# Norm factors moved from the stored rows to the gathered columns, and the residual made by GpSimd during the first experts

## The chip, the cores and the metric

The kernel runs on one core of one Trainium2 chip. The metric is the device time of one execution in microseconds; the median of several executions is compared. The engines are called PE (TensorE matmul), PEld (its weight load), DVE (VectorE), ACT (ScalarE), POOL (GpSimd) and SP (SyncE, which issues most transfers).

## What is computed

One encoder layer over 512 tokens of width 1024, in fp32: a gated DeltaNet mixer, a layer norm, a mixture of experts, a second layer norm and a gated per-token input. The part that matters here:

```
x  = LN(alpha * x + mixer(x))            # first norm: (t - mean) * rstd * g + b
h  = HierMoE(x)                          # top-1 of 4 groups, top-2 of its 8 experts
x  = LN(alpha * x + h)                   # alpha = 2 ** 0.25
x  = x + sigmoid(x Wg) * (p Wp)
```

Each of the 32 experts is `(silu(x Wgate) * (x Wup)) Wdown` with a hidden width of 256.

## The kernel before

**Up to the first norm.** Tokens lie in 4 chunks of 128 rows; `x1[:, c]` is chunk c (128 x 1024). The mixer's output products (`out_products`, L810) for chunk c are added to `x1[:, c]` by DVE (`stats`, L818), which also makes mean and rstd with a chain of very small instructions. `flip_rows` transposes the raw rows on PE (L835) and ACT copies them out (L837); `logits` (L843 to L846) makes the router's logits from raw rows and corrects them by mean and rstd, so routing does not need the normalised rows. `apply` then normalises the rows in place: chunk 1 on DVE with four two-input instructions (L853, L854), chunks 0, 2 and 3 on ACT (L856) followed by four GpSimd instructions each (L859 multiplies by g, L860 adds b; `lng` holds g and b as four broadcast tiles). `store` writes the rows to a DRAM buffer `x1d` and afterwards multiplies `x1` by alpha on ACT (L865), which makes it the residual that the experts' outputs are added to. In this stage a planner orders the instructions of each engine.

**Routing.** Written order on PE, DVE, ACT and POOL: the one-hots of group and experts (L965 to L999), a prefix count on PE (`prk`, L1004), the sort of tokens into 8 passes of 256 slots, and a table on PE (L1077) whose result `gim` gives the row numbers of the gather. `fetch(0)` (L952) gathers 256 rows of `x1d` by two indirect transfers of the POOL queue. `project_p(c)` (L914 to L918), four matmuls, two ACT copies and two stores for chunk c, is work for the last stage that can be put anywhere; `NPJ` says how many chunks come before `prk`, before the first table and before the rest. Then a second, overflow table follows.

**Experts.** Eight passes q = 0 to 7 in a written order on all engines. A pass has 8 up steps and 4 down steps; each step uses one 1 MB weight tile that holds four experts (`w`). Half of a step's matmuls use `w` itself; the other half need a copy of it in an order that the routing decides: `stage` (L1216, L1218) makes it with three DVE copies and one ACT copy of 128 x 512, into two buffers (`ws`). `flip_x` transposes the gathered rows in four parts (PE L1206) and ACT copies each part to `xgT` (L1207). `add` (L1311, DVE) adds the outputs of pass q to the residual `z` (which is `x1`) during the up steps of pass q + 1. `fetch(q + 2)` is issued after the up steps of pass q. Weight tiles rotate through 16 buffers (`ring`, RA + RB); the transfers wait on SP's queue until a buffer comes free.

Of the kernel before, what the change touches and what calls it, by code (L numbers as in the profile page):

```python
# [7 lines left out]
F32 = mybir.dt.float32  # L8
# [3 lines left out]
AF = mybir.ActivationFunctionType  # L12
OP = mybir.AluOpType
# [3 lines left out]
P = 128  # L17
S = 512
D = 1024
KT = 8  # L20
NC_ = 4
NH = 16
NP = 8
ALPHA = 2.0 ** 0.25
# [10 lines left out]
RA = 9  # L35
RB = 7
# [4 lines left out]
R1 = 14  # L41
R0 = 12
NLB = 3
SPE = 'GGGG'
SO = (1, 2, 0, 3)
TE = 'V'
NPJ = (0, 1, 1)
LNV = (1,)
GE = 'GV'
BKK = 4  # L50
BK = 6
# [14 lines left out]
def program(ctx: ExitStack, tc: tile.TileContext, a: dict, out: bass.AP):  # L66
    nc = tc.nc
    V, A, G, T = nc.vector, nc.scalar, nc.gpsimd, nc.tensor
# [14 lines left out]
    x1 = x1p.tile([P, NC_, D], F32, name="x1")  # L83
    lgp = x1p
# [19 lines left out]
    wk = tr.enter_context(tc.tile_pool(name="wk", bufs=2, side="right"))  # L104
    hd = tr.enter_context(tc.tile_pool(name="hd", bufs=4, side="right"))
# [118 lines left out]
    def after(ins, gate, sync=False):  # L224

        cls = mybir.DependencyClass.Sync if sync else mybir.DependencyClass.NoSync
        tc.add_manual_dep(ins.ins, gate.ins.name, mybir.DependencyInfo(cls, mybir.DependencyReason.DATA),
                          reason="order")
# [35 lines left out]
    kcm, qcm, ktm, nv, kkq = {}, {}, {}, {}, {}  # L264
# [323 lines left out]
    def finish(qt, get):  # L588

        ps = (2 * qt, 2 * qt + 1)  # L590
        ms = wk.tile([P, 2, NC_, 2], F32, name="ms")
        scr = wk.tile([P, P], BF16, name="scr", bufs=1)
        for p in ps:
            for c in range(NC_):
                for e in range(2):
                    A.activation(scr, oacc[p][:, c, e], AF.Square, accum_out=ms[:, p % 2, c, e:e + 1])

        for p in ps:
            V.scalar_tensor_tensor(ms[:, p % 2], ms[:, p % 2], 1.0 / P, nq2[:, :, p:p + 1].to_broadcast([P, NC_, 2]),
                                   op0=OP.mult, op1=OP.add)  # L600
        f = wk.tile([P, 2, NC_, 2], F32, name="ff")
        t = wk.tile([P, 2, NC_, 2], F32, name="rq2")
        rsqrt(f, ms, t)
        for p in ps:
            oa = oacc[p]
            G.tensor_tensor(oa, oa, f[:, p % 2, :, :, None].to_broadcast([P, NC_, 2, P]), op=OP.mult)
        for p in ps:
            oa = oacc[p]
            for e in range(2):
                h = 2 * p + e  # L610
                pt = psum.tile([P, NC_, P], F32, name="pmisc", bufs=1)
                for c in range(NC_):
                    T.transpose(pt[:, c], oa[:, c, e], ident)
                zs = wk.tile([P, S], F32, name="zs")
                nc.sync.dma_start(zs, z_dram[h])
                V.scalar_tensor_tensor(zs, pt.rearrange("p c t -> p (c t)"), nw, zs, op0=OP.mult, op1=OP.mult)
                if p not in get():
                    nc.sync.dma_start(oz_dram[h], zs)
                else:
                    oh, ol = get()[p][e]  # L620
                    A.activation(oh, zs, AF.Copy)
                    V.tensor_tensor(ol, zs, oh.bitcast(F32), op=OP.subtract)
            yield
# [115 lines left out]
    wrg = wk.tile([P, KT, 38], F32, name="dc", bufs=3)  # L739
    nc.sync.dma_start(wrg, a["w_rt"])  # L740
    gwr = [wk.tile([P, KT, 36], F32, name="Q") for _ in range(2)]
    for i in range(2):
        V.tensor_tensor(gwr[i], wrg[:, :, 0:36], wrg[:, :, 36 + i:37 + i].to_broadcast([P, KT, 36]), op=OP.mult)
    psg = psum.tile([P, 2, 36], F32, name="ps3", bufs=1)
    for i in range(2):
        for kt in range(KT):
# [19 lines left out]
    for n in range(4):  # L766
        pt_ = wk.tile([P, 256], F32, name="st", bufs=6)
        nc.sync.dma_start(pt_, a["pe_p"][:, 1, 256 * n:256 * n + 256])
        early_p.append(((lambda w, p: w, 1), 256 * n, 256, pt_))
    lng = [hd.tile([P, S], F32, name="kkq", bufs=BKK) for _ in range(4)]  # L770
    for i in range(4):
        nc.sync.dma_start(lng[i], a["ln"][:, i // 2, 512 * (i % 2):512 * (i % 2) + 512].to_broadcast([P, 512]))

    weave((2, finish(3, lambda: {6: o4[0:2], 7: o4[2:4]}), 0, 0, 0.2), (4, split_w2(), 0, 0, 0.5),
          (8 - F7, fl, 0, 0, 1))
# [7 lines left out]
    def ring(shape, dt=F32):  # L783
        nonlocal turn
        turn += 1
        return (ringa if (turn - 1) % (RA + RB) < RA else ringb).tile(shape, dt, name="w")
# [7 lines left out]
    def load():  # L794

        if len(ready) < len(loads):
            ready.append(ring([P, 4, 512]))
            return nc.sync.dma_start(ready[-1], loads[len(ready) - 1])
# [48 lines left out]

    def apply(c, y, nm, ny):

        if c in LNV:  # L850
            for n in range(2):
                ns = slice(512 * n, 512 * n + 512)
                V.scalar_tensor_tensor(x1[:, c, ns], x1[:, c, ns], nm, lng[n], op0=OP.add, op1=OP.mult)  # L853
                V.scalar_tensor_tensor(x1[:, c, ns], x1[:, c, ns], y, lng[2 + n], op0=OP.mult, op1=OP.add)  # L854
        else:
            A.activation(x1[:, c], x1[:, c], AF.Identity, bias=ny, scale=y)  # L856
            for n in range(2):
                ns = slice(512 * n, 512 * n + 512)
                G.tensor_tensor(x1[:, c, ns], x1[:, c, ns], lng[n], op=OP.mult)  # L859
                G.tensor_tensor(x1[:, c, ns], x1[:, c, ns], lng[2 + n], op=OP.add)  # L860

    def store(c):
        stored.append(nc.sync.dma_start(x1d[c * P:(c + 1) * P, :], x1[:, c]))

        A.activation(x1[:, c], x1[:, c], AF.Copy, scale=ALPHA)  # L865

    stored, ps, xT, mo = [], {}, {}, {}
    for i in range(NC_ + 3):
# [15 lines left out]
    tr.close()  # L884
    ringb = rA.enter_context(tc.tile_pool(name="ringb", bufs=RB, side="left", reuse_waits="tile"))
    early = [load() for i in range(RA, R0)]
    for c in SO:
        store(c)
        if R0 > RA:
            after(stored[-1], early[-1])  # L890
    for i in range(max(RA, R0), R1):
        after(load(), stored[-1])
    per = ctx.enter_context(tc.tile_pool(name="per", bufs=1, side="right", reuse_waits="tile"))

    def layernorm(dst, src, gb, pool):
# [52 lines left out]
    def fetch(q):  # L948

        xg = ab_pool.tile([P, 2, D], F32, name="E")  # L950
        for t in range(2):
            i = nc.gpsimd.indirect_dma_start(out=xg[:, t], out_offset=None, in_=x1d[:, :],  # L952
                                         in_offset=bass.IndirectOffsetOnAxis(ap=gim[:, 2 * q + t:2 * q + t + 1], axis=0))
        fetched.append(i)
        return xg
# [139 lines left out]
        project_p(c)  # L1095
    gim, gfm, numbers = table(s128, col, "m", V if TE == "V" else G)
    xg = [fetch(0)]
    for i in range(R1, RA + RB):
        after(load(), fetched[0], True)
    for c in range(NPJ[2], NC_):  # L1100
        project_p(c)
    numbers()


    jf = t32.rearrange("p k c (i e) -> p (k c) i e", i=4)[:, :, :, 0:3]
# [2 lines left out]
                    op=OP.is_ge)  # L1108
# [89 lines left out]
    def flip_x(xg):  # L1198

        xgT = ab_pool.tile([P, KT, 256], F32, name="AT")  # L1200

        def part(k2):
            pt = PT([P, 2, 256], "pmisc" if k2 == 2 else "ps3")
            for i in range(2):
                for t in range(2):
                    T.transpose(pt[:, i, t * P:(t + 1) * P], xg[:, t, (2 * k2 + i) * P:(2 * k2 + i + 1) * P], ident)  # L1206
            A.activation(xgT[:, 2 * k2:2 * k2 + 2], pt, AF.Copy)  # L1207
        return xgT, [lambda k2=k2: part(k2) for k2 in range(4)]

    def stage(w, js):  # L1210

        ws = ek.tile([P, 4, 512], F32, name="ws", bufs=WS)
        for p in range(4):
            src = w[:, bass.ds(js[p], 1)]
            if ROLE[p] == ENG.DVE:
                V.tensor_copy(ws[:, p:p + 1], src)  # L1216
            else:
                A.activation(ws[:, p:p + 1], src, AF.Copy)  # L1218
        return ws

    def quad(ps, l, w, first, last):
        for j in range(4):
# [90 lines left out]
    def overflow(ot):  # L1313
# [3 lines left out]
        with tc.For_i(0, nv_, 1) as i:  # L1317
# [10 lines left out]
            for n in range(2):  # L1328
                pt = PT([P, 4, P], "pmisc")
                for k in range(4):  # L1330
                    T.transpose(pt[:, k], xg[:, (4 * n + k) * P:(4 * n + k + 1) * P], ident)
                A.activation(xt[:, n].rearrange("p (k t) -> p k t", k=4), pt, AF.Copy)
            pg = PT([P, 512], "ps2")
            for k4 in range(2):
                w = (w0, w1)[k4]
# [124 lines left out]
    for q in range(8):  # L1460
        if q == 0:
            man = in_order()
        js = jss[q]
        if q == 0:
            ws = stage(ready[0], js)
        h = up(q, xgT, js, ws, fill)
        parts = []
        if q < 6:
            xg.append(fetch(q + 2))
        if q < 7:  # L1470
            xgT, parts = flip_x(xg.pop(0))
        ws = stage(ready[12 * q + KT], js)
        hT = []
        for x in h:
            hT.append(flip_h(x))
            if parts:
                parts.pop(0)()
        oh = slots(q)
        ys = []
        if q == 7:  # L1480
            parts = [first]
        ws = down(q, hT, js, ws, parts, ys)
        fill = [lambda q=q, c=c, n=n, y=y, oh=oh: add(q, c, n, combine(oh, y, c, "ps1" if q % 2 else "pin"))
                for n, y in enumerate(ys) for c in range(NC_)]
# [104 lines left out]
```

## Time and profile before

| what | value |
|---|---|
| median of 3 runs | 1117.06 us (1114.53 to 1119.78) |
| profiled execution: its own time / its span | 1118.27 us / 1116.5 us |
| PE busy | 1009.3 us, 90% of the span |
| DVE busy | 809.4 us, 72% |
| ACT busy | 548.3 us, 49% |
| POOL busy | 334.3 us, 30% |
| mean granted TensorE clock | 0.942 of full speed |

The profiled execution is 1.2 us above the median. Busy shares are averages over stages with different limits; the stages here are the norm and routing (from about 700 us to 769 us of the span) and the experts (769 us to about 1045 us).

### The profile page before, as it was taken

Reading aid. Unit: us, or ns where it says so; the run is one execution under the profiler, and the core shown is the slowest. Engines: PE = TensorE matmul, PEld = TensorE weight load, DVE = VectorE, ACT = ScalarE, POOL = GpSimd, SP = SyncE. Lnnn points to the kernel's source line nnn. Section 1 sums busy time; section 2 is a strip of 40 time slices with the busy share of each in tenths; the row PEclk is TensorE's granted clock in tenths of the full one; section 3 lists DMA queues with packets and bytes.
Section 4 is the critical chain, followed back from the end, with each engine's and each line's share of the span. In section 5 each row is a group of like instructions: output and inputs, shape, how many; then the busy total and the mean of one; then the engine's idle time right before and its main releaser. Section 6 shows DMA issues by size and latency. Waiting matters only on the chain. (4 is left out here: it accounts for less than half of the span.)

```text
span 1116.5 us, 19701 instructions
## 1 busy us (share of the span) xinstructions
PE 1009.3 (90%) x6954; PEld 703.5 (63%) x6954; DVE 809.4 (72%) x1834; ACT 548.3 (49%) x1406; POOL 334.3 (30%) x273
## 2 busy tenths in 40 slices
PE   9876798977979999989999999958999999999688
PEld 7755677765868887778877888833333333333377
DVE  5889997999894778996556322697666666666784
ACT  3455566655574777556586343224443334432321
POOL 1544534232234344424240274052000000000452
PEclk7988899987999998999999999969999999999789
DMA  4324232121123313223154234878999999970401
GB/s 150 108 66 124 85 98 65 49 57 29 48 90 124 91 58 117 92 77 111 61 161 145 88 123 132 340 274 309 415 420 419 420 406 393 393 319 38 190 28 48
DMA packets 80117, 188.71 MB, mean 169 GB/s; under 512 B 15345, under 2 KB 36849, under 8 KB 67345
## 3 DMA queue, kind: packets, MB, share of 16 engines
q1 hardware_dynamic: 77712, 179.05, 44.1%
q0 software_dynamic: 2304, 8.39, 2.0%
q8 instruction: 55, 0.90, 0.3%
q14 instruction: 46, 0.37, 0.1%
HBM read 174.77 MB, written 12.65 MB: 168 GB/s over the span
## 5 line engine op out<-in xcount | busy, mean ns | idle before, releaser
L240 POOL TENSOR_TENSOR wl<-wr,wh 128x512 fp32r<-128x512 f32 x120 | 160.8, 1343 | 322.8 <-PE pin L243 136.6
L243 PE MATMUL pin<-xh,wh 128*128 128x512 f32 x448 | 137.1, 426 | 36.1 <-DVE cv L257 29.1
L243 PE MATMUL pin<-xl,wh 128*128 128x512 f32 x448 | 135.2, 419 | 0.0
L243 PE MATMUL pin<-xh,wl 128*128 128x512 f32 x448 | 131.2, 412 | 0.3 <-POOL wl L240 0.3
L243 PEld LDWEIGHTS pin<-xh,wh 128*128 128x128 f32 x448 | 86.4, 202 | 57.6 <-DVE cv L257 12.6
L238 ACT ACTIVATE wh<-wr 128x512 fp32r<-128x512 f32 x120 | 75.8, 632 | 92.5 <-PE pin L243 41.2
L1218 ACT ACTIVATE ws<-w 128x512 f32 x96 | 60.5, 630 | 111.8 <-PE ps L1223 57.9
L1216 DVE COPY ws<-w 128x512 f32 x288 | 105.7, 424 | 9.4 <-issue 3.5
L257 DVE SCALAR_TENSOR_TENSOR cv<-pin,cvw,cv 128x510 f32<-128x510 f32 (+1 forms) x128 | 94.4, 741 | 14.8 <-ACT cv L254 14.0
L243 PEld LDWEIGHTS pin<-xl,wh 128*128 128x128 f32 x448 | 89.1, 202 | 19.4 <-DVE xl L642 0.2
L243 PEld LDWEIGHTS pin<-xh,wl 128*128 128x128 f32 x448 | 87.2, 198 | 19.1 <-POOL wl L240 0.7
L952 POOL DMA_INDIRECT E<-x1d,gim x16 | 16.2, 1013 | 170.3 <-PE ps L1206 157.0
L446 POOL TENSOR_TENSOR dc<-dc,negm 128x512 f32<-128x512 f32 x32 | 47.0, 1473 | 44.3 <-DMA dc<-gcd 18.9
L397 DVE TENSOR_TENSOR x<-x,tmp 128x30 f32<-128x30 f32 (+14 forms) x120 | 56.3, 469 | 2.1
L395 DVE TENSOR_TENSOR tmp<-x 128x30 f32<-128x30 f32 (+14 forms) x120 | 53.5, 446 | 2.1
L1311 DVE SCALAR_TENSOR_TENSOR x<-pin,cq,x 128x512 f32<-128x512 f32 x36 | 26.9, 750 | 36.4 <-PE pin L1306 33.0
L448 ACT ACTIVATE dc<-dc,lb 128x128 f32<-128x128 f32 x128 | 41.6, 399 | 15.2 <-POOL dc L446 14.2
L1435 PE MATMUL ps<-w 128*128 128x512 f32 (+1 forms) x192 | 46.4, 405 | 0.0
L542 DVE SCALAR_TENSOR_TENSOR r<-ps,negc,nv 128x128 f32<-128x128 f32 x96 | 29.0, 344 | 23.3 <-PE ps L539 23.1
L1435 PEld LDWEIGHTS ps<-w 128*128 128x128 f32 x192 | 37.5, 206 | 7.6
L1223 PE MATMUL pin<-ws,AT 128*32 128x512 f32 x256 | 39.8, 593 | 0.8 <-DVE ws L1216 0.8
L538 PE MATMUL ps<-st,kcm 128*128 128x256 f32 x96 | 31.7, 413 | 9.6 <-DVE st L570 5.6
(460 smaller groups left out, 2164.7 us busy)
## 6 DMA issues: line engine op xcount, KB each, us to landing
w<-in_w_gu SPq DMA_DIRECT2D x64, 1024.0 KB, 10.0
w<-in_w_dn SPq DMA_DIRECT2D x32, 1024.0 KB, 8.4
wr<-in_w_in SPq DMA_DIRECT2D x96, 256.0 KB, 2.7
dc<-gcd SPq DMA_DIRECT2D x32, 256.0 KB, 3.4
wr<-in_w_out SPq DMA_DIRECT2D x24, 256.0 KB, 3.0
zd<-th SPq DMA_DIRECT2D x16, 256.0 KB, 2.5
zs<-zd SPq DMA_DIRECT2D x16, 256.0 KB, 2.7
w<-in_pe_g SPq DMA_DIRECT2D x6, 512.0 KB, 5.9
```

The costliest lines, as they stand in the source:

```text
L238: A.activation(wh, wr, AF.Copy)
L240: G.tensor_tensor(wl, wr, wh.bitcast(F32), op=OP.subtract)
L243: T.matmul(ps, w[:, k], parts[k0 + k][n], start=(k0 + k + n == 0 and w is wh), stop=(k0 + k == nk_ - 1 and w is wl))
L257: V.scalar_tensor_tensor(y[:, lo:hi], ps[:, lo + j - 2:hi + j - 2], cvw[:, m, j:j + 1], y[:, lo:hi], op0=OP.mult, op1=OP.add)
L395: V.tensor_tensor(t, X[:, m + 1:, m:m + 1].to_broadcast([P, n, m]), X[:, m:m + 1, :m].to_broadcast([P, n, m]), op=OP.mult)
L397: V.tensor_tensor(X[:, m + 1:, :m], X[:, m + 1:, :m], t, op=OP.add)
L446: G.tensor_tensor(dc, dc, negm[:, d:d + 1].to_broadcast([P, 4, P]), op=OP.add)
L448: A.activation(dc[:, u], dc[:, u], AF.Exp, bias=lb[:, c, u0 + u:u0 + u + 1])
L1216: V.tensor_copy(ws[:, p:p + 1], src)
L1218: A.activation(ws[:, p:p + 1], src, AF.Copy)
L1223: T.matmul(ps[32 * j:32 * j + 32], l[:, 32 * j:32 * j + 32], w[:, j], start=first, stop=last, skip_group_check=True)
L1435: T.matmul(pg[n][:, 0:w], x_[:, kt], w_[kt][:, 512 * n + o:512 * n + o + w], start=(kt == 0 and m == 0), stop=(kt == KT - 1 and m == 2))
```

## The change

Rows are normalised by ACT alone, without g and b, for all four chunks, and stored so. The gathered, transposed columns get g and b instead: `gbT` holds them one value per partition, and each part of `flip_x` is copied by two ACT instructions with a scale and a bias in place of one. The g and b rows for the residual are loaded later into one buffer of the weight ring (`lng`), multiplied by alpha by ACT, and GpSimd makes the residual in 16 instructions (`residual`), placed after the up steps and `fetch(2)` in pass 0. `NPJ` goes from (0, 1, 1) to (2, 3, 3).

```diff
-SO = (1, 2, 0, 3)
-NPJ = (0, 1, 1)
-LNV = (1,)
+NPJ = (2, 3, 3)
@@ finish
-        t = wk.tile([P, 2, NC_, 2], F32, name="rq2")
+        t = wk.tile([P, 2, NC_, 2], F32, name="rq2", bufs=1)
@@ before the output products
+    gbT = lgp.tile([P, KT, 2], F32, name="gbT")
+    V.tensor_copy(gbT, wrg[:, :, 36:38])
-    lng = [hd.tile([P, S], F32, name="kkq", bufs=BKK) for _ in range(4)]
-    for i in range(4):
-        nc.sync.dma_start(lng[i], a["ln"][:, i // 2, 512 * (i % 2):512 * (i % 2) + 512].to_broadcast([P, 512]))
@@ apply
-        if c in LNV:
-            for n in range(2):
-                ns = slice(512 * n, 512 * n + 512)
-                V.scalar_tensor_tensor(x1[:, c, ns], x1[:, c, ns], nm, lng[n], op0=OP.add, op1=OP.mult)
-                V.scalar_tensor_tensor(x1[:, c, ns], x1[:, c, ns], y, lng[2 + n], op0=OP.mult, op1=OP.add)
-        else:
-            A.activation(x1[:, c], x1[:, c], AF.Identity, bias=ny, scale=y)
-            for n in range(2):
-                ns = slice(512 * n, 512 * n + 512)
-                G.tensor_tensor(x1[:, c, ns], x1[:, c, ns], lng[n], op=OP.mult)
-                G.tensor_tensor(x1[:, c, ns], x1[:, c, ns], lng[2 + n], op=OP.add)
+        A.activation(x1[:, c], x1[:, c], AF.Identity, bias=ny, scale=y)
@@ store
-        A.activation(x1[:, c], x1[:, c], AF.Copy, scale=ALPHA)
-    for c in SO:
+    for c in range(NC_):
         store(c)
@@ after the stores and two weight loads
+    lng = ring([P, 4, 512])
+    after(nc.sync.dma_start(lng, a["ln"][:, 0:2].rearrange("o k (n w) -> o (k n) w", n=2).to_broadcast([P, 4, 512])),
+          stored[-1])
@@ routing
-    for i in range(R1, RA + RB):
+    for i in range(R1, RA + RB - 1):
         after(load(), fetched[0], True)
     for c in range(NPJ[2], NC_):
         project_p(c)
     numbers()
+    A.activation(lng, lng, AF.Copy, scale=ALPHA)
@@ flip_x
-            A.activation(xgT[:, 2 * k2:2 * k2 + 2], pt, AF.Copy)
+            for i in range(2):
+                kt = 2 * k2 + i
+                A.activation(xgT[:, kt], pt[:, i], AF.Identity, scale=gbT[:, kt, 0:1], bias=gbT[:, kt, 1:2])
+    def residual():
+        for c in range(NC_):
+            for n in range(2):
+                ns = slice(512 * n, 512 * n + 512)
+                G.tensor_tensor(x1[:, c, ns], x1[:, c, ns], lng[:, n], op=OP.mult)
+                G.tensor_tensor(x1[:, c, ns], x1[:, c, ns], lng[:, 2 + n], op=OP.add)
@@ pass loop, after the up steps and the fetch
+        if q == 0:
+            residual()
```

The same scale and bias are applied in the loop for overflowing slots, which has no iterations with these inputs.

## Rows read from the trace of the kernel before

**Rows 1.** Busy time by stretch, in the experts: us, PE, PEld, DVE, ACT, POOL, clock, DMA share, GB/s.

```profile
850.00:900.00 50.00, 49.50 (x360) 18.66 (x363) 33.78 (x78) 20.64 (x39) 2.02 (x2) 1.00 1.01 412
```

**Rows 2.** Busy time by stretch, end of the norm and routing; same columns.

```profile
724.00:728.00 4.00, 4.00 (x36) 3.87 (x35) 4.00 (x6) 3.30 (x6) 3.27 (x3) 1.00 0.21 41
...
744.00:748.00 4.00, 2.35 (x8) 1.32 (x8) 3.65 (x21) 0.00 (x0) 0.00 (x0) 0.50 1.02 373
```

**Rows 3.** Timeline of PE, norm and routing: start, length, engine, line, operation, count.

```profile
729.31 0.63 PE L835 MATMUL ps<-cst,x 128*128 128x128 f32 x4
...
733.56 1.77 PE L843 MATMUL ps<-Q,zs 128*128 128x36 f32 x8
745.65 0.29 PE L1004 MATMUL ps<-ohs,cb 128*128 128x160 bf16 x1 [10.32 <-DVE ohs L999]
...
746.04 6.03 PE L914 MATMUL pin<-E,AT 128*128 128x512 f32 x8
...
753.02 10.55 PE L914 MATMUL pin<-E,AT 128*128 128x512 f32 x24
```

**Rows 4.** Timeline of DVE, last logits to the gather's row numbers.

```profile
736.13 0.26 DVE L846 SCALAR_TENSOR_TENSOR lg<-lg,ly,gs 128x36 f32<-128x36 f32 x1
...
737.42 1.15 DVE L973 TENSOR_TENSOR ohg<-ohg,kmg 128x16 f32<-128x16 f32 x1
738.68 1.25 DVE L978 TENSOR_TENSOR t<-lg,ohg 128x128 f32<-128x128 f32 x1
...
741.12 1.19 DVE L970 TENSOR_TENSOR oh<-oh,ROW 128x32 f32<-128x32 f32 x1
...
744.75 0.19 DVE L973 TENSOR_TENSOR oh<-oh,km 128x32 f32<-128x32 f32 x1
744.98 0.29 DVE L988 TENSOR_TENSOR OH<-ohg,oh 128x128 f32<-128x128 f32 x1
...
753.66 0.17 DVE L1083 CAST gim<-gfm 128x16 int32<-128x16 f32 x1
```

**Rows 5.** Timeline of POOL and of SP's queue, the norm's last instructions and the stores.

```profile
739.73 3.75 POOL L860 TENSOR_TENSOR x<-x,kkq 128x512 f32<-128x512 f32 x3
...
734.69 9.13 SPq L863 DMA_DIRECT2D x1d<-x  x4
```

**Rows 6.** Timeline of DVE and PE, experts, passes 0 and 1.

```profile
781.84 2.10 DVE L1216 COPY ws<-w 128x512 f32 x6 [1.03 <-PE pin L1223]
...
787.49 0.42 DVE L1233 TENSOR_TENSOR h<-h,pin 128x256 f32<-128x256 f32 x1 [1.89 <-ACT h L1232]
...
830.58 1.04 PE L1223 MATMUL ps<-w,hT 128*32 128x512 f32 x8
831.44 1.04 PE L1223 MATMUL ps<-ws,hT 128*32 128x512 f32 x8
```

**Rows 7.** A DVE copy in the mixer: line's shortest, median, longest (ns), and one timeline case.

```profile
L422 DVE COPY x<-x x16: 395/422/1491, 160.5 to 494.8; 32x512 f32<-32x512 f32 x16
...
164.00 1.49 DVE L422 COPY x<-x 32x512 f32<-32x512 f32 x1
...
163.87 1.33 POOL L240 TENSOR_TENSOR wl<-wr,wh 128x512 fp32r<-128x512 f32 x1 [5.10 <-ACT wh L238]
```

**Rows 8.** Timeline of POOL and DVE in the last norm, both back to back.

```profile
1050.08 5.10 POOL L1406 TENSOR_TENSOR w<-w 128x1024 fp32r<-128x1024 f32 x2 [9.86 <-ACT w L1405]
...
1050.13 2.84 DVE L1421 SCALAR_TENSOR_TENSOR x<-x,ly,E 128x512 f32<-128x512 f32 x1
1052.89 2.83 DVE L1420 SCALAR_TENSOR_TENSOR x<-x,mv,E 128x512 f32<-128x512 f32 x1
```

**Rows 9.** ACT copies out of PSUM by shape (busy, mean ns), and a PE wait in flip_x.

```profile
L1207 ACT ACTIVATE AT<-ps 128x512 f32<-128x512 f32 x6 | 3.6, 595 | 1.1 <-PE ps L1206 0.9
...
L1241 ACT ACTIVATE hT<-pmisc 128x256 f32<-128x256 f32 x16 | 6.1, 382 | 2.9 <-PE pmisc L1239 2.8
L304 ACT ACTIVATE kkq<-pmisc,rk 128x128 f32<-128x128 f32 x64 | 18.3, 369 | 5.9 <-PE pmisc L302 5.8
...
858.24 0.66 PE L1206 MATMUL ps<-cst,E 128*128 128x128 f32 x4 [0.21 <-ACT AT L1207]
```

More of the change, by code (lines that the diff above doesn't have):

```diff
@@ L1331, in overflow @@
                     T.transpose(pt[:, k], xg[:, (4 * n + k) * P:(4 * n + k + 1) * P], ident)
-                A.activation(xt[:, n].rearrange("p (k t) -> p k t", k=4), pt, AF.Copy)
+                    kt = 4 * n + k
+                    A.activation(xt[:, n, k * P:(k + 1) * P], pt[:, k], AF.Identity, scale=gbT[:, kt, 0:1],
+                                 bias=gbT[:, kt, 1:2])
             pg = PT([P, 512], "ps2")
```

## Prediction

> **What bounds the kernel now.** I read the busy shares first, then busy time by stretch around the change, then the timelines of all engines from the last output products to the second pass, and last the groups by shape for prices. Two stages matter, and they have different limits.
>
> In the experts PE is the limit: 49.5 of 50 us busy, with the DMA engines full as well and DVE at 33.8 of 50 [rows 1]. What delays PE there delays the end by as much, because no later stage has room to give it back. DVE is the engine closest behind. Each step of an up or down pass takes PE two groups of eight matmuls, 0.86 us apart [rows 6], so 1.72 us, and needs three DVE copies, which run at 2.10 / 6 = 0.35 us each back to back [rows 6]: 1.05 of 1.72 us, with only two `ws` buffers between the engines.
>
> In the norm and routing the limit changes hands. Until 729.9 PE is full (4.00 of 4 us in 724 to 728, [rows 2]; the last transposes of chunk 3 end at 729.31 + 0.63, [rows 3]). From there DVE is the chain: the last logits end at 736.4, the one-hots let PE start `prk` at 745.65 after 10.32 us of idling, and the gather's row numbers are ready at 753.8 [rows 3, 4]. The stores of the rows are not in that chain: the last of the four is issued by 743.8 [rows 5], ten microseconds ahead of the gather. So storing rows earlier is worth nothing by itself; a faster DVE chain is worth its full length, since gather, overflow table and experts follow it in order.
>
> **What the change takes away.** The DVE chain is slowed by GpSimd. While the norm's GpSimd instructions run (3.75 / 3 = 1.25 us each, [rows 5]), DVE instructions with two tensors in SBUF take about the length of one of these more: L973 1.15 us against 0.19 for a larger one undisturbed, L978 1.25 against 0.29 for L988 of its shape, L970 1.19 against about 0.19 [rows 4]. These three alone hold 0.96 + 0.96 + 1.00 = 2.9 us. All twelve GpSimd instructions and the four DVE instructions of chunk 1 go from this place.
>
> Last logits: PE's transposes still end at 729.9. An ACT copy of 0.60 [rows 9], half of the logits' matmuls (1.77 us on a clock that has fallen, [rows 3]; I take 1.2) and two small DVE instructions (0.5) give 732.2, against 736.4. From logits to one-hots it took 745.65 - 736.4 = 9.25 us; less 2.9 that is 6.35, so the one-hots are ready at 738.6.
>
> The new `NPJ` puts eight of the 16 `project_p` matmuls ahead of `prk` on PE. The trace records each twice: 24 records in 10.55 us are three chunks at full clock, 3.5 us each; 8 records in 6.03 us are one chunk at half clock [rows 3], where the granted clock was 0.50, the lower of the two levels (1.2 GHz), after PE had idled [rows 2, 3]. Two chunks from 731.7 on end at 738.8 at full clock and at 743.8 at half. PE comes to them straight from full work, so I take full clock: `prk` at 738.8 instead of 745.65, **6.9 us gained**. The bounds are 1.9 (half clock) and 8.0 (PE done first, one-hots at 737.6). After `prk` nothing on the chain changes; the other chunks fit into waits there. The one ACT instruction on `lng`, the `gbT` copy, the four g and b loads that leave SP's queue and the later load of `lng` stand ahead of nothing that waits: I cost them at nothing. The weight ring loses a buffer for its first turn; a load that was issued 16 steps ahead is issued 15 ahead, some 25 us before it is needed. If transfers were late the cover would be gone, but PE shows no wait on a weight tile.
>
> **What it adds: the column factors.** Each part of `flip_x` is one ACT copy of 0.597 us; it becomes two of 128 x 256. The trace has a plain one at 0.382 and a scaled one of 128 x 128 at 0.369, which at (0.597 - 0.382) / 256 us per element makes 0.476 for 256 [rows 9]. So a part takes 0.76 to 0.95 us, 0.17 to 0.36 more. PE waits for just this copy once in every pass (0.21 us before the second part's transposes, [rows 9]), so the addition lands on PE: eight flips, 1.4 to 2.9 us. I take **2 us lost**.
>
> **What it adds: the residual.** Sixteen GpSimd instructions of 1.25 us, 20.1 us together, start behind `fetch(2)` about halfway through pass 0's up steps. They are off PE's path, but behind the shared access to SBUF stands DVE. A DVE copy like `stage`'s, single input, SBUF to SBUF, takes 0.42 us and was held to 1.49 when a GpSimd instruction ran from 163.87 to 165.20: it ended 0.3 us behind it [rows 7]. Copies, not only two-input instructions, are blocked. Where both engines had work back to back they took turns: two GpSimd instructions of 2.4 us side by side with DVE's L1421 and L1420, each 2.83 instead of 0.75 or so [rows 8]. Behind the blocked copy on DVE stand the other two of its step, and PE waits for them.
>
> If they take turns one for one, the residual needs 16 x (1.25 + 0.42) = 26.7 us, in which DVE makes 16 copies, 5.33 steps, worth 9.2 us of PE: 17.5 us lost. Between up and down DVE has nothing to copy (idle 1.89 us and a product that reads PSUM, [rows 6]); two GpSimd instructions pass free there, 2.5 us. That leaves **15 us lost**. The bounds: 0, if GpSimd only fills DVE's idle time, and 20.1, if nothing overlaps.
>
> Of this the Trainium skill, SBUF — State Buffer, section "Who interferes with whom", says that a DVE instruction in a two-port mode and a GpSimd instruction exclude each other for the whole instruction, and that issue order decides who waits. By that rule the three copies of a step, if they are issued together, could all go ahead of the next GpSimd instruction; the sum would then be that of the third rival below. [Rows 8] speak for one for one, with two-input instructions; no row shows copies back to back against GpSimd back to back.
>
> **The sum.** From the profiled execution: 1118.3 - 6.9 + 2 + 15 = 1128.4. It stands 1.2 above the median, so the median should come to **1127**. Over bounds: losses of 10 to 17.5 and gains of 4 to 8 make 1121 to 1134, the likeliest case's own range.
>
> **Rivals.**
> 1. *The residual costs nothing* (not slower). GpSimd gets its turns in DVE's idle time, 16 of 50 us [rows 1], and the copies keep PE fed. For it: DVE has this idle time. Against it: [rows 7], a GpSimd instruction once started holds a copy up, and GpSimd has nothing that paces it. Time: 1117.1 - 6.9 + 2 = 1112. It decides as soon as the residual costs PE less than 4.9 us.
> 2. *The routing gain fails too.* The clock falls before the projections and they hold `prk` back: gain 1.9. For it: half clock at that very place before [rows 2]. Against it: that came after PE had idled, and now it has work. Time: 1117.1 - 1.9 + 2 + 15 = 1132.
> 3. *Three copies for each GpSimd instruction.* The residual stretches to 16 x (1.25 + 1.05) = 36.8 us, in which DVE makes 48 copies, 16 steps, 27.5 us of PE: 9.3 lost, less 2.5 at the turn: 6.8. Time: 1117.1 - 6.9 + 2 + 6.8 = 1119. The page named above would allow it.
>
> **Chances.** My forecast 0.55, rival 1 0.22, rival 2 0.10, rival 3 0.13. A measurement of this kernel can tell about 0.5%, 5.6 us, from no change: under 1111.5 is faster, over 1122.6 slower. Rival 1 lies at the edge and is split: 0.12 faster, 0.10 same. Rival 3 is the same in 0.11. The forecast's lower end gives 0.04 to the same. A residue of 0.02 goes to faster, for a routing chain that loses more than I count. That makes 0.14 faster, 0.25 same, 0.61 slower. The range of 8 in 10 reaches from 1111, which leaves out the better half of rival 1, to 1135.
>
> **What the profile would show.** Gain: no GpSimd instruction between 724 and 744, no DVE instruction of routing over 0.6 us but the large one-hots, `prk` near 739, `gim` near 747, the first up matmul near 762. Flip: two ACT instructions of 0.4 to 0.5 us per part, PE's wait at the second part 0.4 to 0.6. Residual: sixteen GpSimd instructions in about 27 us, `stage` copies of some 1.6 us among them, steps of about 5 us on PE where they were 1.7, and then the old rhythm. I am wrong if those copies stay near 0.4 us, or if GpSimd's instructions are the ones that stretch, to several microseconds each.

## The result, and the profile after

The changed kernel takes 1127.62 us (median of nine runs, 1119.53 to 1129.81) against 1117.06 us before (nine runs, 1114.53 to 1120.45). The ratio is 1.0081, with a 95% interval of 1.0055 to 1.0106: slower, by about 9 us. Its profiled execution has an own time of 1128.93 us and a span of 1127.1 us.

In both profiled executions the last output product of the mixer starts on PE at nearly the same moment (724.4 before, 724.3 after), so times from there on can be set side by side. The marks, from the timelines of DVE and PE:

| mark | before | after | difference |
|---|---|---|---|
| last logits ready | 736.4 | 735.7 | -0.7 |
| `prk` starts | 745.65 | 740.94 | -4.7 |
| row numbers `gim` | 753.66 | 749.09 | -4.6 |
| first up matmul of pass 0 | 768.96 | 763.82 | -5.1 |
| first matmul that brings pass 0's outputs back (L1306, after L1307) | 800.55 | 807.19 | +6.6 |
| last group of such matmuls, last pass | 1046.56 | 1055.88 | +9.3 |
| end of the span | 1116.5 | 1127.1 | +10.6 |

So routing gained 5.1 us, pass 0 lost 11.8, the other seven passes lost 2.7, and the last stage 1.3. The border between the first two scatters: the first up matmul comes 39.5 us after the last output product here (44.5 before), but 40.9 to 41.0 in a_no_residual, f_half, i_skew and j_same_op, whose routing is the same.

**Routing.** Busy time by stretch of the changed kernel (us, PE, PEld, DVE, ACT, POOL, clock, DMA share, GB/s), to be read beside [rows 1, 2]:

```profile
724.00:728.00 4.00, 4.00 (x31) 3.39 (x30) 3.14 (x14) 4.00 (x7) 0.00 (x0) 1.00 0.00 0
...
740.00:744.00 4.00, 3.06 (x12) 1.63 (x12) 3.69 (x23) 0.72 (x2) 0.00 (x0) 1.00 0.97 321
748.00:752.00 4.00, 3.91 (x13) 1.84 (x14) 2.11 (x14) 0.00 (x0) 1.56 (x2) 0.50 1.01 415
776.00:798.00 22.00, 17.39 (x96) 4.24 (x88) 20.73 (x17) 8.49 (x16) 21.35 (x17) 1.00 0.90 349
850.00:900.00 50.00, 49.17 (x348) 18.66 (x340) 31.84 (x73) 19.05 (x37) 2.02 (x2) 1.00 0.99 401
```

GpSimd is gone from the norm (0.00 us in 724 to 728). In 776 to 798, while GpSimd makes the residual, PE is busy for 17.39 of 22 us only. Timeline of PE in the changed kernel, answering to [rows 3]:

```profile
727.12 3.60 PE L904 MATMUL pin<-E,AT 128*128 128x512 f32 x8
...
735.79 3.70 PE L904 MATMUL pin<-E,AT 128*128 128x512 f32 x8 [0.69 <-ACT ws L907]
740.94 0.23 PE L994 MATMUL ps<-ohs,cb 128*128 128x160 bf16 x1 [1.44 <-DVE ohs L989]
...
763.82 1.94 PE L1224 MATMUL pin<-w,AT 128*32 128x512 f32 x8 [1.20 <-ACT AT L1200]
```

Timeline of DVE from the last logits, answering to [rows 4]:

```profile
735.43 0.26 DVE L844 SCALAR_TENSOR_TENSOR lg<-lg,ly,gs 128x36 f32<-128x36 f32 x1
...
736.72 0.17 DVE L963 TENSOR_TENSOR ohg<-ohg,kmg 128x16 f32<-128x16 f32 x1
737.00 0.38 DVE L968 TENSOR_TENSOR t<-lg,ohg 128x128 f32<-128x128 f32 x1
...
749.09 0.17 DVE L1073 CAST gim<-gfm 128x16 int32<-128x16 f32 x1
```

The same instructions that took 1.15 and 1.25 us in [rows 4] take 0.17 and 0.38. But a `project_p` chunk (727.12, 3.60 us) now stands on PE among the last transposes and logits, so the last logits come hardly earlier than before. From them to `prk` it takes 5.3 us where it took 9.25.

**Pass 0.** Timeline of POOL in the changed kernel (the first three and the last of the sixteen residual instructions):

```profile
776.19 1.29 POOL L1219 TENSOR_TENSOR x<-x,w 128x512 f32<-128x512 f32 x1
777.56 1.34 POOL L1220 TENSOR_TENSOR x<-x,w 128x512 f32<-128x512 f32 x1
778.86 1.44 POOL L1219 TENSOR_TENSOR x<-x,w 128x512 f32<-128x512 f32 x1
...
797.21 1.32 POOL L1220 TENSOR_TENSOR x<-x,w 128x512 f32<-128x512 f32 x1
```

Timelines of DVE (nine copies in one row, then a copy out of that row in a narrower stretch) and of PE in the same time:

```profile
775.80 13.29 DVE L1209 COPY ws<-w 128x512 f32 x9 [1.73 <-PE pin L1224]
...
777.70 1.49 DVE L1209 COPY ws<-w 128x512 f32 x1
...
779.24 1.05 PE L1224 MATMUL pin<-ws,AT 128*32 128x512 f32 x2 [0.36 <-DVE ws L1209]
780.64 0.62 PE L1224 MATMUL pin<-ws,AT 128*32 128x512 f32 x2 [0.36 <-DVE ws L1209]
```

A copy begins soon after a GpSimd instruction and ends 0.29 us behind it (777.70 + 1.49 = 779.19, against 777.56 + 1.34 = 778.90). The copies end 1.4 us apart, each GpSimd instruction gives way to one of them, and PE waits for each copy in turn. A step of three copies takes PE 4.2 us in place of 1.7.

**The flips.** Group of the new ACT instructions (shortest, median, longest in ns), then rows of the timelines of ACT, PE and POOL; the PE row answers to the last of [rows 9], the POOL rows are the fetches of two passes:

```profile
L1200 ACT ACTIVATE AT<-ps,gbT x48: 548/562/576, 763.2 to 1014.4; 128x256 f32<-128x256 f32 x48
...
864.70 1.02 ACT L1200 ACTIVATE AT<-ps,gbT 128x256 f32<-128x256 f32 x2
...
865.77 0.66 PE L1197 MATMUL ps<-cst,E 128*128 128x128 f32 x4 [0.64 <-ACT AT L1200]
...
805.68 1.05 POOL L942 DMA_INDIRECT E<-x1d,gim  x1 [7.15 <-PE ps L1197]
...
840.42 0.94 POOL L942 DMA_INDIRECT E<-x1d,gim  x1 [32.32 <-PE ps L1197]
```

A part takes ACT 1.02 us instead of 0.60, and PE's wait grows from 0.21 to 0.64 us. The pass takes 840.42 - 805.68 = 34.74 us; before, fetches stand at 799.04 and 833.34, 34.30 apart.

### The profile page after: what moved, and what is told of

The parts are those of the page before. It is cut to its first block, busy times and chain, and to the rows that moved or that the text cites. A ratio compares the mean times of both kernels' runs of the same rounds, so it can differ in the third digit from the quotient of the medians.

```text
span 1127.1 us, 19735 instructions
## 1 busy us (share of the span) xinstructions
PE 1017.3 (90%) x6954; PEld 704.0 (62%) x6954; DVE 812.9 (72%) x1831; ACT 560.5 (50%) x1436; POOL 342.1 (30%) x277
## 3 DMA queue, kind: packets, MB, share of 16 engines
q1 hardware_dynamic: 77280, 179.05, 44.5%
## 5 line engine op out<-in xcount | busy, mean ns | idle before, releaser
L1209 DVE COPY ws<-w 128x512 f32 x288 | 118.8, 469 | 8.9 <-ACT ws L1211 4.8
L393 DVE TENSOR_TENSOR tmp<-x 128x30 f32<-128x30 f32 (+14 forms) x120 | 56.3, 469 | 2.1
L1312 DVE SCALAR_TENSOR_TENSOR x<-pin,cq,x 128x512 f32<-128x512 f32 x36 | 26.9, 750 | 37.2 <-PE pin L1307 34.3
L1312 DVE SCALAR_TENSOR_TENSOR x<-ps,cq,x 128x512 f32<-128x512 f32 x28 | 20.8, 749 | 25.6 <-PE ps L1307 25.6
```

What stands on the lines that cost most here:

```text
L393: V.tensor_tensor(t, X[:, m + 1:, m:m + 1].to_broadcast([P, n, m]), X[:, m:m + 1, :m].to_broadcast([P, n, m]), op=OP.mult)
L1312: V.scalar_tensor_tensor(z[:, c, ns], pc, cq[:, q, c:c + 1], z[:, c, ns], op0=OP.mult, op1=OP.add)
```

## The experiments

Ratios are to the kernel before, timed alongside on the same chip.

**a_no_residual.** The changed kernel without the residual's instructions.

```diff
-        if q == 0:
-            residual()
```

> The changed kernel without its sixteen GpSimd instructions; this leaves the factors g, b and alpha out of the residual. Theory 1 (GpSimd's instructions hold up the DVE copies of pass 0 and PE waits for them): pass 0 of the experts loses some 11 us in the changed kernel (5.1 us ahead of the kernel before at its first matmul, 6.6 us behind it at the first matmul of pass 1), so this kernel takes 1116 to 1117 us, about the time of before. Theory 2 (the residual is hidden and the loss comes from the weight ring that is one buffer short, or from the transfer into it): both are still here, so 1126 to 1129 us, and DVE copies in pass 0 as long as in the changed kernel.

1117.70 us, ratio 0.9995 (0.9973 to 1.0016). By time the residual is the whole loss: without it the rest of the change balances to nothing. Against the changed kernel that is 0.86%, 9.6 us. In the trace pass 0, from its first up matmul to the first matmul that brings its outputs back, takes 31.1 us; in the changed kernel 43.4.

**b_npj.** The old placement of the projections.

```diff
-NPJ = (2, 3, 3)
+NPJ = (0, 1, 1)
```

> The changed kernel with the projections spread as before, NPJ = (0, 1, 1). Theory 1 (the planner put the first chunk's projection ahead of the logits of chunks 2 and 3 on PE, 3.4 us, and this took back half of the routing gain): the last logits are ready near 732.3 instead of 735.7, the prefix count starts near 737.5 instead of 740.9, and the time is 1123 to 1125 us. Theory 2 (without this work PE's granted clock falls to 0.5, and the projections that come later run at half speed and hold up the table): the prefix count starts earlier, but the gather's row numbers do not, and the time is 1127 to 1130 us.

1124.42 us, ratio 1.0063 (1.0038 to 1.0088). PE's timeline: the last logits' matmuls, and `prk` behind them with nothing between:

```profile
731.19 1.08 PE L841 MATMUL ps<-Q,zs 128*128 128x36 f32 x8
738.11 0.29 PE L994 MATMUL ps<-ohs,cb 128*128 128x160 bf16 x1 [5.84 <-DVE ohs L989]
738.51 6.25 PE L904 MATMUL pin<-E,AT 128*128 128x512 f32 x8
```

Counted from the last output product, `prk` starts 2.7 us earlier than in the changed kernel (13.9 against 16.6 us), although PE idles 5.84 us and its granted clock falls to 0.50 (736 to 740): the next chunk takes 6.25 us where it took 3.70. The first up matmul comes 3.1 us earlier. So the new `NPJ` took back some 3 us of the routing gain, by putting a projection in front of the logits. By time the two kernels are not told apart (their intervals overlap).

**c_one_copy.** One plain ACT copy per part in the flips, as before.

```diff
-            for i in range(2):
-                kt = 2 * k2 + i
-                A.activation(xgT[:, kt], pt[:, i], AF.Identity, scale=gbT[:, kt, 0:1], bias=gbT[:, kt, 1:2])
+            A.activation(xgT[:, 2 * k2:2 * k2 + 2], pt, AF.Copy)
```

> The changed kernel with one plain ACT copy for each part of the flipped columns, as before; this leaves g and b out of what the experts see. Theory 1 (the second part's transposes wait for the first part's copy in every pass, 0.64 us instead of 0.21): a pass takes 34.3 us instead of 34.74, and the time is about 3 us less, 1124 to 1125.5 us. Theory 2 (the wait only moves, and the columns cost nothing at the end): a pass stays at 34.7 us, 1127 to 1128 us.

1126.98 us, ratio 1.0063 (1.0036 to 1.0091): above the expected range by its median, and not told from the changed kernel by time. In the trace the pass is back at 34.3 us, and the last pass ends 2.9 us earlier, counted from the last output product.

**d_act_copies.** In pass 0 ACT makes three of the four `ws` copies, DVE one (the engine that loads each copy's index changes with it and is left out of the cut below).

```diff
+    ROLE0 = (ENG.Activation, ENG.Activation, ENG.DVE, ENG.Activation)
-            if ROLE[p] == ENG.DVE:
+            if (ROLE0 if js is jss[0] else ROLE)[p] == ENG.DVE:
```

> The changed kernel with three of the four copies of each step in pass 0 made by ACT and one by DVE, instead of one and three. Theory 1 (one GpSimd instruction goes for each DVE copy): with one DVE copy a step, the residual no longer sets the step; ACT does, 3 x 0.63 = 1.9 us a step where PE needs 1.72. Pass 0 loses 3 to 6 us instead of 11, and the time is 1119 to 1123 us. Theory 2 (something else than the DVE copies delays pass 0): more ACT work only adds, 1128 to 1133 us.

1121.86 us, ratio 1.0034 (1.0013 to 1.0056). Busy time by stretch during the residual (columns as above):

```profile
770.00:792.00 22.00, 18.85 (x168) 6.63 (x164) 15.74 (x15) 21.08 (x41) 18.53 (x15) 1.00 0.99 387
```

Pass 0 takes 33.65 us instead of 43.4, with the residual still in it. That the residual reaches PE through DVE's copies is shown by this; ACT, now 21.08 of 22 us busy, is probably the next limit. The profiled execution lost part of it ahead of pass 0 (first up matmul 42.7 us after the last output product, 39.5 in the changed kernel).

**e_bank.** The second part of a flip goes into a PSUM buffer that is free at that time, so that its transposes don't wait for the first part's copy.

```diff
-            pt = PT([P, 2, 256], "pmisc" if k2 == 2 else "ps3")
+            alt = "pin" if q is not None and q % 2 else "ps1"
+            tag = "pmisc" if k2 == 2 else alt if k2 == 1 or k2 == 3 and q is None else "ps3"
+            pt = PT([P, 2, 256], tag)
```

> The changed kernel with the second part of each flip transposed into a PSUM buffer that is free at that time, so that it needn't wait for the first part's copy (in the flip ahead of pass 0, the fourth part too). Theory 1 (that wait, 0.64 us in each pass where it was 0.21 before, is the whole price of the column factors): a pass goes from 34.74 to 34.1 us, the time is 3 to 4.5 us less, 1123 to 1124.5 us. Theory 2 (ACT is what the flip waits for, and PE then waits at the next place, the copy of the hidden values): a pass stays at 34.7, 1127 to 1128 us.

1123.68 us, ratio 1.0061 (1.0039 to 1.0082). The pass takes 33.9 us, less than before the change, when PE still waited 0.21 us: PE's wait, and not ACT's longer work as such, is what the flips cost. The time does not price this alone. Here the residual starts at 768.14, while DVE still has routing to finish, and PE then waits 11.20 us for a `ws` copy; pass 0 takes 45.0 us against 43.4. It is the collision that g_combo meets again below.

**f_half.** The residual with its eight multiplications alone.

```diff
-                G.tensor_tensor(x1[:, c, ns], x1[:, c, ns], lng[:, 2 + n], op=OP.add)
```

> The changed kernel with only the eight multiplications of the residual, without its eight additions; this leaves alpha times b out of the residual. Theory 1 (every GpSimd instruction takes one turn from the DVE copies): half of the instructions cost half, about 5 us of the 10 that leaving out all sixteen gave back, 1121 to 1123 us. Theory 2 (the cost is in starting the residual at that place, not in its length): nearly as in the changed kernel, 1126 to 1128 us; or, if the turn between up and down hides most of eight instructions, 1118 to 1119 us.

1126.74 us, ratio 1.0088 (1.0061 to 1.0115). The theory of turns, by which half the instructions cost half, put the end of its range 3.7 us lower. The time lies in the range of theory 2, but its reason (the start, not the length) does not hold: one copy is held for just as long as the series lasts, and sixteen such instructions cost far more (h_two_runs). Timelines of POOL, DVE and PE:

```profile
773.91 9.82 POOL L1219 TENSOR_TENSOR x<-x,w 128x512 f32<-128x512 f32 x8
...
773.52 10.49 DVE L1209 COPY ws<-w 128x512 f32 x1
...
784.07 1.40 PE L1223 MATMUL pin<-ws,AT 128*32 128x512 f32 x3 [7.62 <-DVE ws L1209]
```

There are no turns here. What differs is that no multiplication depends on the one ahead of it, while each addition of the changed kernel does; and that the operation never changes.

**h_two_runs.** The same sixteen instructions, multiplications first.

```diff
-        for c in range(NC_):
-            for n in range(2):
-                ns = slice(512 * n, 512 * n + 512)
-                G.tensor_tensor(x1[:, c, ns], x1[:, c, ns], lng[:, n], op=OP.mult)
-                G.tensor_tensor(x1[:, c, ns], x1[:, c, ns], lng[:, 2 + n], op=OP.add)
+        for o, op in ((0, OP.mult), (2, OP.add)):
+            for c in range(NC_):
+                for n in range(2):
+                    ns = slice(512 * n, 512 * n + 512)
+                    G.tensor_tensor(x1[:, c, ns], x1[:, c, ns], lng[:, o + n], op=op)
```

> The changed kernel, with the residual as eight multiplications one after another and then eight additions, instead of multiplication and addition in turn; the same result. Theory 1 (a VectorE copy gets its turn only where the next GpSimd instruction depends on the one before): VectorE copies are held for some 10 us twice, and the kernel takes 1128 to 1137 us, not less than the changed kernel. Rival (a copy gets its turn after every GpSimd instruction in either order): 1126 to 1128 us as the changed kernel, with no copy held over 2 us.

1138.07 us, ratio 1.0188 (1.0138 to 1.0238). Timelines of POOL, DVE and PE:

```profile
776.33 19.57 POOL L1220 TENSOR_TENSOR x<-x,w 128x512 f32<-128x512 f32 x16
...
775.95 20.24 DVE L1209 COPY ws<-w 128x512 f32 x1
...
796.25 1.40 PE L1224 MATMUL pin<-ws,AT 128*32 128x512 f32 x3 [17.37 <-DVE ws L1209]
```

That is 1 us above theory 1's range. It is one hold of 20.24 us and not the two of ten that were expected: at the one change from multiplication to addition the copy got no turn either. GpSimd is quicker (19.57 against 22.3 us) and the kernel slower.

**i_skew and j_same_op.** Two orders that separate dependence from the change of operation. i_skew runs multiplication k, then addition k - 1; j_same_op keeps the order of the changed kernel but only multiplies.

```diff
# i_skew
+        for k in range(9):
+            for i, o, op in ((k, 0, OP.mult), (k - 1, 2, OP.add)):
+                if 0 <= i < 8:
+                    c, n = divmod(i, 2)
+                    ns = slice(512 * n, 512 * n + 512)
+                    G.tensor_tensor(x1[:, c, ns], x1[:, c, ns], lng[:, o + n], op=op)
# j_same_op
-                G.tensor_tensor(x1[:, c, ns], x1[:, c, ns], lng[:, 2 + n], op=OP.add)
+                G.tensor_tensor(x1[:, c, ns], x1[:, c, ns], lng[:, 2 + n], op=OP.mult)
```

> The changed kernel, with each addition of the residual placed one multiplication later: multiplication 1, addition 0, multiplication 2, addition 1 and so on; the same result. Each GpSimd instruction but the ends is then of another operation than the one ahead of it, and none depends on that one. Theory 1 (a VectorE copy gets its turn only while a GpSimd instruction waits for the result of the one just ahead): one copy is held for 15 to 20 us and the kernel takes 1134 to 1139 us as with all multiplications first. Rival (a change of the operation lets the copy in): 1126 to 1129 us as the changed kernel, no copy held over 2 us.

> The changed kernel, with the eight additions of the residual replaced by multiplications of the same tiles and operands, which leaves alpha times b out of the residual and makes it wrong by that factor. Each second GpSimd instruction depends on the one just ahead, and all have the same operation. Theory 1 (dependence lets the copy in): 1126 to 1129 us as the changed kernel, no copy held over 3 us. Rival (a change of the operation lets it in): a copy held for 15 to 20 us, 1134 to 1139 us.

i_skew: 1137.82 us, ratio 1.0180 (1.0134 to 1.0225). j_same_op: 1127.60 us, ratio 1.0101 (1.0066 to 1.0136). Timelines of POOL and DVE of i_skew:

```profile
774.77 19.55 POOL L1221 TENSOR_TENSOR x<-x,w 128x512 f32<-128x512 f32 x16
...
774.38 20.23 DVE L1209 COPY ws<-w 128x512 f32 x1
```

The group of all copies of j_same_op (shortest, median, longest in ns):

```profile
L1209 DVE COPY ws<-w x288: 406/420/1999, 760.4 to 1043.2; 128x512 f32 x144
```

Alternating operations without dependence hold a copy for 20.23 us; dependent pairs of one operation hold none over 2 us. So for these copies it is dependence on the instruction just ahead, and not a change of operation, that gives the turns. A dependent instruction here also works on the same stretch of `x1` as the one ahead; the runs don't separate the two.

**g_combo.** b, d and e together, with the written order starting ahead of the first flip (`man = in_order()` moved up).

> The changed kernel with NPJ = (0, 1, 1), the free PSUM buffer for the second part of each flip, three of the four copies of each step of pass 0 on ACT, and the written order begun ahead of the first flip, so that its ACT copies no longer stand behind a weight copy that waits for the projections' stores. Theory 1 (the three losses lie in series and add up): 2.5 us from the projections, 3 to 4 from the flips, 5 to 6 from the copies and 1 to 2 from the first flip, so 1112 to 1115 us, below both kernels. Theory 2 (ACT, which now does the columns and three copies in pass 0, becomes the limit there and gives none of it, and the flips' gain is lost in pass 0): 1118 to 1121 us.

1117.54 us, ratio 1.0010 (0.9988 to 1.0032): 2.5 us above the expected range, no gain over the kernel before. Timelines of POOL, DVE and PE:

```profile
763.93 1.28 POOL L1222 TENSOR_TENSOR x<-x,w 128x512 f32<-128x512 f32 x1
...
763.79 1.46 DVE L1160 CAST ei<-ef 128x16 int32<-128x16 f32 x1
...
772.05 1.22 DVE L1180 SCALAR_TENSOR_TENSOR c<-sq__7835,c 128x64 f32<-128x64 f32 x1
...
776.18 1.07 PE L1227 MATMUL pin<-ws,AT 128*32 128x512 f32 x2 [5.64 <-DVE ws L1212]
```

With all flips done early, the fetch and the residual start at 761.7 and 763.9, while DVE still has routing to finish. Nine of its small instructions are now held for 1.0 to 1.5 us each, the copies stand behind them, and pass 0 takes 42.3 us.

**g2_gate.** g_combo with the residual's first instruction waiting for the last routing instruction of DVE.

```diff
-    V.tensor_add(cq, c8[:, 1, :, 0:4], c8[:, 1, :, 4:8])
+    cqi = V.tensor_add(cq, c8[:, 1, :, 0:4], c8[:, 1, :, 4:8])
-                G.tensor_tensor(x1[:, c, ns], x1[:, c, ns], lng[:, n], op=OP.mult)
+                i = G.tensor_tensor(x1[:, c, ns], x1[:, c, ns], lng[:, n], op=OP.mult)
+                if c + n == 0:
+                    after(i, cqi, True)
```

> As g_combo, but the first GpSimd instruction of the residual waits for the last VectorE instruction of the routing. Theory 1 (the two streams collided in g_combo: GpSimd's residual began while VectorE still had routing work before the first copies): the collision goes, pass 0 is back from 42.3 us to about the 33.7 us of d_act_copies, and the kernel takes about 1108 to 1111 us, 0.5 to 0.8% below the kernel before. Rival (the collision only moves into the first weight copies, which VectorE then makes late): 1114 to 1118 us, no different from the kernel before.

1110.21 us, ratio 0.9915 (0.9883 to 0.9946): faster than the kernel before. Timelines of POOL and PE:

```profile
768.89 1.53 POOL L1222 TENSOR_TENSOR x<-x,w 128x512 f32<-128x512 f32 x1 [3.21 <-DVE cq L1182]
...
763.32 1.07 PE L1229 MATMUL pin<-w,AT 128*32 128x512 f32 x8 [0.34 <-ACT AT L1203]
...
798.25 1.19 PE L1314 MATMUL pin<-y,oh 128*128 128x512 f32 x4
```

The residual starts 5 us later than in g_combo and pass 0 is back at 798.25 - 763.32 = 34.9 us. So the change pays in this company: the residual no longer meets DVE's routing and meets one DVE copy a step instead of three. How much of the 0.85% is the change's own is not shown, since the PSUM buffer and the earlier written order could be given to the kernel before too, and it was not run with them.

## Why the prediction came out

The forecast was 1127 with "slower" as the likeliest case, and 1127.62 was measured. Its mechanism held: a copy for each GpSimd instruction, PE waiting behind the copies. That the number is so near is luck: three terms were off and a fourth was missing, with both signs. By the marks the profiled executions give -5.1 + 11.8 + 2.7 + 1.3 = 10.7 us; the prediction's terms were -6.9 + 2 + 15 = 10.1.

- **Routing, -6.9 forecast.** At `prk` 4.7 us came, 5.1 at the first up matmul. The step that failed is "last logits at 732.2": they were ready at 735.7, since a projection went ahead of them on PE. b_npj, without it, has them 8.7 us after the last output product, against 11.4 in the changed kernel and 7.8 in the forecast; so the projection took 2.7 us, and 0.9 is open. It was not the clock of rival 2: the granted clock was 1.00 until 744. The other step was better than forecast: 5.3 us from logits to `prk` where 6.35 was expected. Freed of GpSimd, DVE gained 4 us there, not 2.9. Two more of its instructions had been held before, which the forecast did not count: L967 (0.58 us at 740.50) and the L973 below; each takes 0.19 now.

```profile
742.56 0.97 DVE L973 TENSOR_TENSOR oh<-oh,km 128x32 f32<-128x32 f32 x1
```

- **Flips, 2 forecast.** An instruction takes 0.562 us, over the 0.38 to 0.476 that I took from the plain copy and from the 128 x 128 shape, so a part grew by 0.42 us and not by 0.17 to 0.36. Seven passes lost 2.7 us in the marks; in pass 0 the residual hides what the flip adds. The 369 ns of the scaled shape in [rows 9] carry one per-partition operand, the new instructions two. The Trainium skill, ScalarE: Activation LUTs, section "What ACT_TABLE_LOAD costs", says that each such operand adds about 93 ns. On the plain copy's 0.382 that would have made an estimate of 0.568; the trace agrees with 0.562.
- **Residual, 15 forecast.** It cost 9.6 us by the ratios with and without it. By the traces it cost 10.9: from the last output product to the first matmul that brings pass 0's outputs back it takes 82.9 us in the changed kernel and 72.0 in a_no_residual. The term was mis-sized at the length of a turn: not 1.25 + 0.42 = 1.67 us but 1.41, so the two overlap by 0.26. With that the prediction's own working gives 22.6 us in place of 26.7, still 16 copies worth 9.2 us of PE, and 22.6 - 9.2 - 2.5 = 10.9. That this meets the measured 10.9 so exactly is luck as well: in that time DVE made 13 copies and not 16, and two one-hots (L1269) were held too.
- **Rivals.** Rival 1 (nothing) is out by a_no_residual. Rival 3 (three copies for each GpSimd instruction) is out by the trace: nine copies need 13.29 us.
- **The last stage, not in the sum.** It took 1.3 us more. There GpSimd and DVE work side by side as in [rows 8], and in the changed kernel the norm's 128 x 1 instructions on DVE are the ones held. The timeline of DVE has three such in a row, of which this is one; before, the same three took 0.16 to 0.22 us and two large ones were held instead:

```profile
1058.05 2.26 DVE L280 SCALAR_TENSOR_TENSOR ly<-lt,ly 128x1 f32<-128x1 f32 x1
```

All the other variants of the changed kernel show a longer last stage too, by 1.3 to 1.8 us. What sets that alignment was not tried.

## What to carry to other kernels

Before moving work to GpSimd, look at what DVE does in that stretch and who waits for it: an instruction on GpSimd that is off the path can still put its own length on a DVE instruction beside it, and on PE if PE waits for that. Here copies and many small instructions were held; a product that reads PSUM was not (L1234, 0.41 us at 789.01). If the two must overlap, give DVE's share of that stretch to ACT, or start GpSimd behind the DVE work that is most urgent; g2_gate did both, with the old `NPJ`, a free PSUM buffer and an earlier first flip beside them, and the loss of 0.8% became a gain of 0.85%. The order of GpSimd's own instructions counts too: the same sixteen took the kernel to 1127.62 us in dependent pairs and to 1138.07 in two runs. And a per-partition scale and bias in a copy is not free: time the exact shape and operands, or take the transposes behind it to another PSUM buffer.

## What the runs showed of the hardware

How long a DVE copy of this kernel (128 x 512, one input, SBUF to SBUF) is held by GpSimd depends on the order in which GpSimd's instructions depend on one another. With every second instruction dependent on the one ahead, a copy got in after each (1.41 us a turn, no hold over 2.0). With none dependent on its predecessor, a single copy was held for the whole series: 10.49 us for eight, 20.24 and 20.23 us for sixteen. It is curious that with dependent pairs the copies also got in between pairs, where nothing depends; why was not tried.

This does not hold for every DVE instruction. In the last norm of the changed kernel GpSimd's instructions are independent as well (`split_wg`: each reads and writes tiles of its own) and follow one another without a gap, yet a 128 x 1 instruction of DVE got in after each of them. Whether these small instructions with several inputs or that GpSimd series make the difference was not tried. Timelines of POOL and DVE; the first DVE row is the one that follows 1058.05 above:

```profile
1060.26 4.64 POOL L1409 TENSOR_TENSOR w<-w 128x1024 fp32r<-128x1024 f32 x2
...
1060.35 2.27 DVE L279 SCALAR_TENSOR_TENSOR lt<-ly,lx 128x1 f32<-128x1 f32 x1
1062.65 2.26 DVE L280 SCALAR_TENSOR_TENSOR ly<-lt,ly 128x1 f32<-128x1 f32 x1
```

The Trainium skill, SBUF — State Buffer, section "Who interferes with whom", says that the two exclude each other for a whole instruction and that issue order decides who waits. The first half agrees with the holds. The second does not cover these: the held copies were recorded as starting at 775.95 and 774.38, ahead of the first residual instruction (776.33, 774.77), and all sixteen still went before them. In g2_gate the first meeting did go by order: the copy at 768.87 took its 0.43 us, and the GpSimd instruction at 768.89 took 1.53 us where the first of the changed kernel's series took 1.29.

Small instructions can be held just as long: a 128 x 16 cast for 1.46 us in g_combo (0.18 in the changed kernel), 128 x 1 for 2.26 us in the last norm.
